# A mixture-of-experts stage whose large and small experts run block by block in turns

## The chip, the cores and the metric

The kernel runs on one core of a Trainium2 chip, as one program. The metric is the time of one execution on the device, in microseconds (us). Before the change three executions took 1911.71, 1914.14 and 1914.71 us.

## What is computed

A network of two blocks over 256 tokens of width 1024: two hybrid attention layers, then two mixer layers, the first with a dense feed-forward part and the last with a mixture of experts. The change touches only that last part:

```python
def swiglu(x, w_gate, w_up, w_down):
    return (jax.nn.silu(x @ w_gate) * (x @ w_up)) @ w_down

def moe_swiglu(x, router_w, w_gate, w_up, w_down):
    logits = (x @ router_w).astype(jnp.float32)
    top_v, top_i = lax.top_k(logits, TOP_K)
    gates = jax.nn.softmax(top_v, axis=-1)
    combine = jnp.sum(jax.nn.one_hot(top_i, N_EXPERTS, dtype=jnp.float32) * gates[..., None], axis=-2)
    y = jnp.zeros_like(x)
    for e in range(N_EXPERTS):
        y = y + combine[..., e:e + 1].astype(x.dtype) * swiglu(x, w_gate[e], w_up[e], w_down[e])
    return y
```

There are 8 experts, each token goes to 2 of them, the inner width is 3584, and all is float32.

## The kernel before, in words

The stage starts some 1000 us into the run, and everything ahead of it stays as it is. The router's counts rank the experts at run time. The program works on eight places `e`: the even ones are large experts (up to 128 tokens), the odd ones small (up to 64, `FEW`). A few tokens too many for their place would go through `overflow`, behind a branch.

The inner width is cut into 7 blocks `b` of 512 columns. A block needs six pieces of weights of 1 MB: two each of gate, up and down. They are loaded by SyncE (SP) in the order of the program (`raw_unit`, L378) into a ring of some 14 buffers, one ahead of the other, each as soon as its buffer's last reader is done.

A large block (`proj`, `down`) keeps float32 accuracy by splitting: `weights` has ScalarE (ACT) round a piece to the high part `whi` (L417, three buffers), and VectorE (DVE) subtract it for the low part (L418). TensorE (PE) then runs three matmuls for each product: L1858, L1859 (high part of the weights with the tokens' high and low part) and L1864 for gate and up; L1932, L1933 and L1935 for down. A small block (`proj_few`, L1877, and the odd branch of `down`, L1918) uses the float32 weights as they come, two matmuls side by side in 64 columns each of the array, with nothing to split.

Between the projections and `down` lies a chain. For a small block ACT copies the result out of PSUM (`act`, L1883), PE transposes it (`turn`, L1893), ACT applies silu (L1898), DVE multiplies (L1899). A large block has silu on ACT (L1885) and a product on DVE (L1886) ahead of the transposes, and a cast on ACT (L1903) and a difference on DVE (L1904) behind them.

`gather` picks an expert's tokens by matmuls with a one-hot matrix (L1767) and copies them to SBUF (`gh`, `gl`; `fx` for the small expert). `scatter` brings an expert's result back to token order (L1951, L1952) and adds it to `y` on DVE (L1954).

The blocks run expert by expert, in one loop over `blocks`; in each step the projections of a block are issued together with `turn` and `down` of the block before. A scheduler in the framework then fixes each engine's order when the program is built, by priorities (`ahead`) and by what it takes to be ready; on the chip each engine keeps that order.

```python
blocks = [(e, b) for e in range(NE) for b in range(7)]
```

Of the kernel before, what the change touches and what calls it, by code (L numbers as in the profile page):

```python
# [11 lines left out]
F32 = mybir.dt.float32  # L12
# [4 lines left out]
ALU = mybir.AluOpType  # L17
# [5 lines left out]
KC = 8  # L23
# [4 lines left out]
NE = 8  # L28
# [3 lines left out]

RANKS = (None, 3, 0, 4, 1, 5, 2, 6)
FEW = 64

SPLITS = (("dsa_q", 256), ("dsa_k", 64), ("dsa_v", 64), ("idx_q", 256), ("idx_k", 32), ("idx_w", 8),
          ("fox_q", 384), ("fox_k", 384), ("fox_v", 384), ("fox_f", 6), ("nsa_q", 384), ("nsa_kc", 128),
# [243 lines left out]
class Net:  # L281
# [1393 lines left out]
    def _moe(self, x, out):  # L1675
        nc, d, hw, tc = self.nc, self.d, self.hw, self.tc
# [63 lines left out]
        def back(oh, dt):  # L1740

            ohf = oh.bitcast(F32) if dt is F32R else oh
            oht = self.late.tile([128, NE, T], dt, name="oht", tag="oht")
            for e in range(0, NE, 2):
                p = self.psum("o")
                for i in range(2):
                    for tb in range(2):
                        t = nc.tensor.transpose(p[:, i * 256 + tb * 128:i * 256 + tb * 128 + 128], ohf[:, tb, e + i], self.ident)
                        self.after(t, gm)
                i = nc.scalar.copy(oht[:, e:e + 2], p.rearrange("p (e t) -> p e t", e=2))  # L1750
                self.after(i, gx)
            return oht

        gh, gl = (own(n).rearrange("p (k s) -> p k s", k=KC) for n in ("gh", "gl"))

        fx = hw.tile([128, KC, FEW], F32, name="fx")

        def gather(qs, tags="ot", low=nc.vector.tensor_copy):

            q = qs[0]  # L1760
            for k in range(0, KC, 2):
                for src, dst, ev, tag in ((xh, gh, nc.scalar.copy, tags[0]), (xl, gl, low, tags[1])):
                    p = self.psum(tag)
                    for i in range(2):
                        for tb in range(2):
                            o = oh[:, tb, q:q + 2] if len(qs) == 2 else oh[:, tb, q][:, None].to_broadcast([128, 2, 128])
                            last = nc.tensor.matmul(p[:, i * 256:i * 256 + 256],  # L1767
                                                    src[:, tb, (k + i) * 128:(k + i) * 128 + 128], o, start=tb == 0,
                                                    stop=tb == 1)
                    p = p.rearrange("p (k s) -> p k s", k=2)  # L1770
                    at = slice(0 if ev == nc.scalar.copy and q else (128 * (q > 0)), 256 if len(qs) == 2 else 128)
                    if at.start < at.stop:
                        kept[ev == nc.vector.tensor_copy] = ev(dst[:, k:k + 2, at], p[:, :, at])
                    if q and src is xl:
                        nc.vector.tensor_tensor(fx[:, k:k + 2], p[:, :, 0:FEW], gh[:, k:k + 2, 0:FEW].bitcast(F32), op=ALU.add)
                yield
            self.hold = kept[0], kept[1] or self.hold[1], None
            kept[2] = last

        b1 = b  # L1780
        early = [[(None, i0)] * 3 + [(None, b)], (None, b)]
        late, kept = kept, [None] * 3
        with self.ahead(5000):
            for _ in gather((0,), ("mm", "mm"), nc.scalar.copy):
                pass
        gx, gm = kept[0], kept[2]
        for cs, p in late:
# [53 lines left out]
        def block_of(n, q, b, hf):  # L1841

            if q == 0:
                return d[n][0, b, hf]
            return d[n][bass.ds(expert[q], 1), b, hf].rearrange("e p n -> (e p) n")
# [2 lines left out]

        def proj(e, b, n, steps=iter(())):

            es = slice(128 * (e > 0), 128 * (e > 0) + 128)
            p = self.psum()
            for hf in range(2):
                w = block_of(n, e, b, hf)
                h, lo = self.weights(w, hold=early.pop(0), pieces=range(4)) if early else self.weights(w)
                for i in range(4):
                    k, cs = hf * 4 + i, slice(i * 512, i * 512 + 512)
                    nc.tensor.matmul(p, gh[:, k, es], h[:, cs], start=k == 0, stop=False)  # L1858
                    nc.tensor.matmul(p, gl[:, k, es], h[:, cs], start=False, stop=False)  # L1859
                if hf:  # L1860
                    next(steps, None)
                for i in range(4):
                    k, cs = hf * 4 + i, slice(i * 512, i * 512 + 512)
                    nc.tensor.matmul(p, gh[:, k, es], lo[:, cs], start=False, stop=k == KC - 1)  # L1864
                next(steps, None) if hf == 0 else None
            PP[e, b, n] = p

        def proj_few(e, b, hf):

            p = PP[e, b] = PP.pop((e, b)) if hf else self.psum()  # L1870
            with self.ahead(3000):
                ws = [self.passing(block_of(n, e, b, hf)) for n in ("mgate", "mup")]
            for i in range(4):
                k = hf * 4 + i
                for r, w in enumerate(ws):
                    r *= FEW
                    nc.tensor.matmul(p[r:r + FEW], fx[:, k], w[:, i * 512:i * 512 + 512], start=k == 0, stop=k == KC - 1,  # L1877
                                     tile_position=(0, r), skip_group_check=True)

        def act(e, b):  # L1880
# [8 lines left out]
        def turn(e, b):  # L1889
            sg = H.pop((e, b))  # L1890
            pt = self.psum("t")
            for i in range(4):
                nc.tensor.transpose(pt[:, i * 128:i * 128 + 128], sg[:, i * 128:i * 128 + 128], self.ident)  # L1893
            if e % 2:
                pv = pt.rearrange("p (f m) -> p f m", f=4)

                fs, fh = sg.rearrange("p (a f m) -> a p f m", a=2, f=4)
                nc.scalar.activation(fs, pv[:, :, 0:FEW], AF.Silu)  # L1898
                nc.vector.tensor_tensor(fh, fs, pv[:, :, FEW:], op=ALU.mult)  # L1899
                H[e, b] = fh  # L1900
                return
            hh, hl = mh[:, (7 * e + b) % 2, 0], mh[:, (7 * e + b) % 2, 1]
            nc.scalar.copy(hh, pt)  # L1903
            nc.vector.tensor_tensor(hl, pt, hh.bitcast(F32), op=ALU.subtract)  # L1904
            H[e, b] = hh, hl

        def down(e, b, steps=iter(())):
            if b == 0:
                YD[e] = [self.psum("s") for _ in range(1 if e % 2 else 2)]
            yd = YD[e]  # L1910
            if e % 2:
                fh = H.pop((e, b))
                for hf in range(2):
                    with self.ahead(3000):
                        w = self.passing(block_of("mdown", e, b, hf))
                    for i, c in product(range(2), range(2)):
                        f, r = hf * 2 + i, FEW * c
                        nc.tensor.matmul(yd[0][r:r + FEW], fh[:, f], w[:, i * 1024 + c * 512:i * 1024 + c * 512 + 512],  # L1918
                                         start=b == 0 and f == 0, stop=b == 6 and f == 3, tile_position=(0, r),
                                         skip_group_check=True)  # L1920
# [20 lines left out]
                self.split(yh, yl, p)  # L1941
                H[e, "y", c] = yh, yl

        def scatter(e, tags="oooo"):
            for c in range(2):
                yh, yl = H.pop((e, "y", c)) if e % 2 == 0 else H[e, "y", 0]
                r = slice(FEW * c, FEW * c + FEW) if e % 2 else slice(0, 128)
# [7 lines left out]
                                                   op1=ALU.add)  # L1955

        mh = None
        blocks = [(e, b) for e in range(NE) for b in range(7)]
        for n, (e, b) in enumerate(blocks):
            if n == 4:  # L1960
                with tc.issue_after(self.load.ins):
                    for q in range(1, NE):
                        r = RANKS[q]
                        expert[q] = nc.values_load(idi[0:1, r:r + 1], engines=(mybir.EngineType.SP,), min_val=1, max_val=NE - 1)
            if n == 9:

                mc = hw.tile([128, 1], F32, name="mc")
# [14 lines left out]
                mh = hw.tile([128, 2, 2, 512], F32R, name="mh", tag="mh")  # L1982
            if n:
                turn(*blocks[n - 1])
            if e % 2:
                proj_few(e, b, 1)
            else:
                if b == 6:
                    steps = gather((e + 1, e + 2)[:NE - 1 - e])
                proj(e, b, "mup", steps)  # L1990
            act(e, b)
            if n:
                down(*blocks[n - 1], steps)
            for _ in steps:
                pass
            if b == 1 and e:
                scatter(e - 1)
            if n == len(blocks) - 5:
                gb = self.rows()
        with self.ahead(4000):  # L2000
            turn(*blocks[-1])
        down(*blocks[-1])
        scatter(NE - 1, ("t", "o", "s", "s"))


        with tc.issue_after(self.load.ins):
# [10 lines left out]
    def rows(self):  # L2017

        nc = self.nc
        r = self.px.tile([1, 2, D], F32, name="rows", tag="x")  # L2020
        nc.gpsimd.dma_start(r, self.d["rows"][None])
        gb = self.xp.tile([128, 2, D], F32, name="gb", tag="xlo")
        for i, c in product(range(2), range(2)):
            p = self.psum("o")
            nc.tensor.matmul(p, self.ones[0:1], r[:, i, c * 512:c * 512 + 512], start=True, stop=True)
            nc.scalar.copy(gb[:, i, c * 512:c * 512 + 512], p)
        return gb
# [112 lines left out]
```

## Time and profile before

| | us |
|---|---|
| median of three executions | 1914.14 |
| profiled execution | 1920.84 |
| its span in the trace | 1919.1 |
| PE busy in the span | 1845.0 (96%) |
| DVE, ACT busy | 1072.9 (56%), 873.5 (46%) |
| loads of weights on SP's queue, share of 16 engines | 66.4% |

Busy times of PE are of pipelined matmuls whose ends are modelled, so that a busy PE need not be at its peak. The granted clock of PE is given as a share of 2.4 GHz; 0.5 of it is the 1.2 GHz level. Each time in the rows below counts from the span's start.

### The profile page before, as it was taken

How to read it: one execution, taken by the hardware profiler on the slowest of the kernel's cores; microseconds unless marked ns; L12 is line 12 of the kernel's file. 1: busy time of each engine (PE TensorE's matmuls, PEld its weight loads, DVE VectorE, ACT ScalarE, POOL GpSimd, SP SyncE). 2: the span in 40 equal slices, each digit the busy share in tenths (PEclk: the TensorE clock that was granted, in tenths of full speed). 3: DMA queues.
4: the chain of work that ended last, by engine and by line, in shares of the span. 5: the costliest groups of instructions: out<-in, count | busy, mean ns of one | idle time of the engine just before them, and what ended most of it. 6: DMA issues, size and time to landing. Idle time of an engine off the chain costs nothing. (4 is left out here: it accounts for less than half of the span.)

```text
span 1919.1 us, 27033 instructions
## 1 busy us (share of the span) xinstructions
PE 1845.0 (96%) x10708; PEld 1363.4 (71%) x10708; DVE 1072.9 (56%) x1582; ACT 873.5 (46%) x1295; POOL 32.9 (2%) x71
## 2 busy tenths in 40 slices
PE   7999999999999999999989999999999999999996
PEld 5777788879888998798877863478436873478532
DVE  3765687765546654555359850388306962278402
ACT  3464465545454543444537740367205751267311
POOL 1000000000000000000000000000000000000000
PEclk9999999999999999899989999999999999999998
DMA  9655443234113555441266989999899999999886
GB/s 390 240 208 198 175 144 111 89 123 154 45 66 132 176 183 190 144 154 48 86 263 253 358 328 390 422 421 401 325 416 422 421 373 360 421 421 415 301 347 258
DMA packets 71173, 497.66 MB, mean 259 GB/s; under 512 B 8226, under 2 KB 9538, under 8 KB 11264
## 3 DMA queue, kind: packets, MB, share of 16 engines
q1 hardware_dynamic: 70752, 495.39, 66.4%
q8 instruction: 86, 1.41, 0.3%
q0 software_dynamic: 288, 0.48, 0.1%
q14 instruction: 47, 0.39, 0.1%
HBM read 493.81 MB, written 1.05 MB: 258 GB/s over the span
## 5 line engine op out<-in xcount | busy, mean ns | idle before, releaser
L418 DVE TENSOR_TENSOR raw<-raw,whi 128x2048 fp32r<-128x2048 f32 (+1 forms) x165 | 297.9, 1823 | 188.8 <-ACT whi L417 187.8
L417 ACT CAST whi<-raw 128x2048 fp32r<-128x2048 f32 (+1 forms) x191 | 292.7, 1557 | 145.8 <-PE mm L439 48.6
L438 PE MATMUL mm<-xhi,whi 128*128 128x256 f32 x720 | 182.1, 288 | 0.7 <-ACT whi L417 0.7
L1858 PE MATMUL mm<-whi,gh 128*128 128x512 f32 x448 | 176.8, 395 | 6.1 <-ACT whi L417 6.1
L417 ACT CAST whi<-room 128x2048 fp32r<-128x2048 f32 (+1 forms) x97 | 171.7, 1804 | 23.5 <-PE mm L1859 7.2
L439 PE MATMUL mm<-xlo,whi 128*128 128x256 f32 x720 | 180.4, 286 | 0.0
L1859 PE MATMUL mm<-whi,gl 128*128 128x512 f32 x448 | 175.6, 392 | 0.0
L1877 PE MATMUL mm<-room,fx 128*64 128x512 f32 x544 | 161.0, 595 | 3.0 <-DMA room<-in_mup_dram 1.8
L418 DVE TENSOR_TENSOR room<-room,whi 128x2048 fp32r<-128x2048 f32 x62 | 142.0, 2290 | 19.5 <-ACT whi L417 16.9
L1899 DVE TENSOR_TENSOR msg<-msg,t 128x256 f32<-128x256 f32 x28 | 11.8, 420 | 237.6 <-ACT msg L1898 237.6
L438 PEld LDWEIGHTS mm<-xhi,whi 128*128 128x128 f32 x720 | 137.6, 191 | 8.1 <-issue 5.6
L439 PEld LDWEIGHTS mm<-xlo,whi 128*128 128x128 f32 x720 | 137.7, 191 | 1.5 <-issue 1.4
L1883 ACT COPY msg<-mm 128x512 f32<-128x512 f32 x28 | 16.4, 585 | 233.3 <-PE mm L1877 233.3
L1877 PEld LDWEIGHTS mm<-room,fx 128*64 128x64 f32 x544 | 48.3, 137 | 87.5 <-issue 79.3
L443 PE MATMUL mm<-xhi,raw 128*128 128x256 f32 x720 | 104.2, 285 | 0.0
L1858 PEld LDWEIGHTS mm<-whi,gh 128*128 128x128 f32 x448 | 84.4, 188 | 27.7 <-ACT whi L417 10.1
L1859 PEld LDWEIGHTS mm<-whi,gl 128*128 128x128 f32 x448 | 84.6, 189 | 17.7
L443 PEld LDWEIGHTS mm<-xhi,raw 128*128 128x128 f32 x720 | 93.6, 191 | 1.2 <-DVE cin L1199 0.9
L1932 PE MATMUL s<-whi,mh 128*128 128x512 f32 x224 | 90.1, 403 | 3.4 <-ACT whi L417 3.4
L1933 PE MATMUL s<-whi,mh 128*128 128x512 f32 x224 | 90.3, 404 | 0.0
L1877 PE MATMUL mm<-raw,fx 128*64 128x512 f32 x232 | 87.1, 609 | 2.3 <-DMA raw<-in_mup_dram 2.3
L1864 PE MATMUL mm<-room,gh 128*128 128x512 f32 x236 | 65.1, 396 | 0.4 <-DVE room L418 0.4
(597 smaller groups left out, 3469.5 us busy)
## 6 DMA issues: line engine op xcount, KB each, us to landing
room<-in_mgate_dram SPq DMA_DIRECT2D x67, 1024.0 KB, 11.4
room<-in_mup_dram SPq DMA_DIRECT2D x64, 1024.0 KB, 10.1
raw<-in_mdown_dram SPq DMA_DIRECT2D x51, 1024.0 KB, 12.1
room<-in_mdown_dram SPq DMA_DIRECT2D x49, 1024.0 KB, 11.7
raw<-in_mup_dram SPq DMA_DIRECT2D x30, 1024.0 KB, 10.2
raw<-in_win_dram SPq DMA_DIRECT2D x29, 1024.0 KB, 6.5
raw<-in_mgate_dram SPq DMA_DIRECT2D x28, 1024.0 KB, 9.4
raw<-in_din_dram SPq DMA_DIRECT2D x24, 1024.0 KB, 4.8
```

The source lines that it names most:

```text
L417: a = nc.scalar.copy(h[:, v], r[:, v])
L418: b = nc.vector.tensor_tensor(lo[:, v], r[:, v], h[:, v].bitcast(F32), op=ALU.subtract)
L438: nc.tensor.matmul(out, w, xh[:, k], start=start and i == 0, stop=False)
L439: nc.tensor.matmul(out, w, xl[:, k], start=False, stop=False)
L443: nc.tensor.matmul(out, lo[:, off + i * 128:off + i * 128 + 128], xh[:, k], start=False, stop=stop and i == n - 1)
L1858: nc.tensor.matmul(p, gh[:, k, es], h[:, cs], start=k == 0, stop=False)
L1859: nc.tensor.matmul(p, gl[:, k, es], h[:, cs], start=False, stop=False)
L1864: nc.tensor.matmul(p, gh[:, k, es], lo[:, cs], start=False, stop=k == KC - 1)
L1877: nc.tensor.matmul(p[r:r + FEW], fx[:, k], w[:, i * 512:i * 512 + 512], start=k == 0, stop=k == KC - 1, tile_position=(0, r), skip_group_c ...
L1883: nc.scalar.copy(sg, PP.pop((e, b)))
L1932: nc.tensor.matmul(yd[c], hh[:, fs], h[:, ws], start=b == 0 and f == 0, stop=False)
L1933: nc.tensor.matmul(yd[c], hl[:, fs], h[:, ws], start=False, stop=False)
```

## The change

Large and small experts are paired: after two blocks of the first large expert, a small block and a large block follow in turns until the end. What goes with it: the small experts' tokens `fx` get two buffers, a large expert always uses the first half of `gh`, the small experts' `down` accumulates in the PSUM bank `o`, and `gather`, `scatter`, `back` and `rows` use the four shared banks `mm` in place of `o` and `t`. The registers with the experts' numbers are loaded at the second block and not at the fifth. No matmul, cast or load is added or left out.

```diff
+BEHIND = 2
...
-        def gather(qs, tags="ot", low=nc.vector.tensor_copy):
+        FX = {}
+        def gather(q, tags="mm", low=nc.vector.tensor_copy, some=True, few=True):
+            if few:
+                fx = FX[q + 1] = hw.tile([128, KC, FEW], F32, name="fx", tag="fx", bufs=2)
+            at = slice(0 if some else 128, 256 if few else 128)
...
-            es = slice(128 * (e > 0), 128 * (e > 0) + 128)
+            es = slice(0, 128)
...
         def down(e, b, steps=iter(())):
             if b == 0:
-                YD[e] = [self.psum("s") for _ in range(1 if e % 2 else 2)]
+                YD[e] = [self.psum("o")] if e % 2 else [self.psum("s") for _ in range(2)]
...
-        def scatter(e, tags="oooo"):
+        def scatter(e, tags=("mm",) * 4):
...
-        blocks = [(e, b) for e in range(NE) for b in range(7)]
+        many, few = ([(e, b) for e in range(i, NE, 2) for b in range(7)] for i in range(2))
+        blocks = many[:BEHIND]
+        for i in range(len(few)):
+            blocks += [few[i], *many[BEHIND + i:BEHIND + i + 1]]
         for n, (e, b) in enumerate(blocks):
-            if n == 4:
-                with tc.issue_after(self.load.ins):
-                    for q in range(1, NE):
+            if n == 1:
+                for q in range(1, NE):
...
+            if n + 1 == BEHIND:
+                steps = gather(0, some=False)
...
-                if b == 6:
-                    steps = gather((e + 1, e + 2)[:NE - 1 - e])
+                if b == 6 and e + 2 < NE:
+                    steps = gather(e + 2)
...
-            if b == 1 and e:
-                scatter(e - 1)
+            if n > 2 and blocks[n - 2][1] == 6:
+                scatter(blocks[n - 2][0])
```

First place: PE around the transposes of a small block, in a run of small blocks before. `fx` marks the projections, `msg` with 64 columns `down`, `lead` the transposes.

```order
L1877 MATMUL mm<-x,fx 64x512
L1877 MATMUL mm<-raw_10976,fx 64x512
L1918 MATMUL s<-raw_10988,msg 64x512 x4
L1893 MATMUL t<-lead,msg 128x128 x4
L1918 MATMUL s<-raw_10994,msg 64x512 x4
L1877 MATMUL mm<-room_11001,fx 64x512
```

The same place after the change, where the lines stand some ten further down: `room_10897` and `room_10899` are the last weights of a small block's projections, L1943, L1944 and L1946 the `down` of the large block before it.

```order
L1886 MATMUL mm<-room_10897,fx 64x512
L1886 MATMUL mm<-room_10899,fx 64x512
L1902 MATMUL t<-lead,msg 128x128 x4
L1943 MATMUL s<-whi,mh 128x512
L1944 MATMUL s<-whi,mh 128x512
```

Four matmuls of `down` stood between a small block's last projection and its transposes; now nothing does, and the large block's `down` comes behind them.

Second place: ACT in a run of small blocks before.

```order
L1883 COPY msg<-mm 128x512
L1898 ACTIVATE msg<-t 128x256
L1883 COPY msg<-mm 128x512
L1898 ACTIVATE msg<-t 128x256
L417 CAST whi<-room_11185 128x2048
```

ACT after the change, one pair of blocks: the last two casts of a large block's up weights, its silu and the cast behind its transposes, then the small block's copy, and on either side of the small block's silu the casts of the large block's down weights.

```order
L418 CAST whi<-xlo 128x2048
L418 CAST whi<-raw_10844 128x2048
L1894 ACTIVATE msg<-mm 128x512
L1913 CAST mh<-t 128x512
L1892 COPY msg<-mm 128x512
L418 CAST whi<-x 128x2048
L1907 ACTIVATE msg<-t 128x256
L418 CAST whi<-raw_10929 128x2048
```

The casts that the large block's `down` waits for have come to stand behind a copy that waits for the small block's last projection. This holds for 26 of the 28 pairs.

Third place: PE at the end of a large block's up projection after the change. L1867, L1868 and L1873 are the three products, L1929 is the `down` of the small block before.

```order
L1867 MATMUL mm<-whi,gh 128x512
L1868 MATMUL mm<-whi,gl 128x512
L1929 MATMUL o<-raw_10865,msg 64x512
L1873 MATMUL mm<-xlo,gh 128x512 x4
L1929 MATMUL o<-raw_10865,msg 64x512 x3
L1929 MATMUL o<-room_10871,msg 64x512 x4
```

One of the eight matmuls of the small `down` is cut off from the other seven by the low products; this stands 22 times in the program. Before, a run of small blocks kept the eight in two fours.

## Rows read from the trace of the kernel before

**Rows 1.** The page, part 1: busy us (share of span) x instructions of each engine.

```profile
PE 1845.0 (96%) x10708; PEld 1363.4 (71%) x10708; DVE 1072.9 (56%) x1582; ACT 873.5 (46%) x1295; POOL 32.9 (2%) x71
```

**Rows 2.** Busy time by stretch: stretch, its length, each engine, then PE clock, DMA share, GB/s.

```profile
1262.34:1330.13 67.79, 67.79 (x305) 55.62 (x304) 60.74 (x33) 48.55 (x32) 0.00 (x0) 1.00 1.01 417
1384.76:1428.91 44.15, 44.15 (x210) 15.11 (x209) 1.68 (x4) 3.87 (x8) 0.00 (x0) 1.00 1.01 417
...
1262.34:1484.33 221.99, 214.89 (x946) 131.17 (x944) 117.60 (x83) 95.47 (x77) 0.00 (x0) 0.99 0.98 395
```

**Rows 3.** Waits of PE from 1000 us on: total us, times, longest.

```profile
PE o L1951 <- DVE y L1954: 6.3, 7, 0.9
PE mm L1858 <- ACT whi L417: 6.1, 5, 1.6
PE s L1932 <- ACT whi L417: 3.4, 3, 1.1
PE t L1893 <- ACT msg L1883: 2.8, 4, 0.7
PE mm L1877 <- DMA raw<-in_mup_dram: 2.3, 2, 1.4
PE mm L1877 <- DMA room<-in_mup_dram: 1.8, 2, 0.9
```

**Rows 4.** Timeline of PE, change to the last small expert: start, us, work, [idle before <-releaser].

```profile
1803.25 1.02 PE L1877 MATMUL mm<-room,fx 128*64 128x512 f32 x2
1804.95 0.66 PE L1893 MATMUL t<-lead,msg 128*128 128x128 f32 x4 [0.68 <-ACT msg L1883]
1806.75 0.50 PE L1932 MATMUL s<-whi,mh 128*128 128x512 f32 x1 [1.14 <-ACT whi L417]
...
1809.07 1.20 PE L1935 MATMUL s<-xlo,mh 128*128 128x512 f32 x4 [0.19 <-DVE xlo L418]
1810.11 0.40 PE L1932 MATMUL s<-whi,mh 128*128 128x512 f32 x1
```

**Rows 5.** Timeline of ACT, the same place.

```profile
1804.31 0.59 ACT L1883 COPY msg<-mm 128x512 f32<-128x512 f32 x1 [6.43 <-PE mm L1877]
1804.79 1.90 ACT L417 CAST whi<-room 128x2048 fp32r<-128x2048 f32 x1
```

**Rows 6.** Timeline of PE, change to the second small expert.

```profile
1355.68 3.65 PE L1877 MATMUL mm<-room,fx 128*64 128x512 f32 x16
1360.05 0.66 PE L1893 MATMUL t<-lead,msg 128*128 128x128 f32 x4 [0.71 <-ACT msg L1883]
...
1366.30 0.40 PE L1932 MATMUL s<-whi,mh 128*128 128x512 f32 x1
...
1384.76 0.66 PE L1893 MATMUL t<-lead,msg 128*128 128x128 f32 x4
```

**Rows 7.** Stretches behind three such changes, PE alone: granted clock, DMA share, GB/s.

```profile
1807.00:1810.00 3.00, 2.81 (x12) 1.00 0.80 298
...
1362.00:1365.00 3.00, 3.00 (x8) 0.52 0.98 396
1585.00:1587.00 2.00, 2.00 (x6) 0.50 0.98 397
```

**Rows 8.** Timeline of PE, change from a small to a large expert.

```profile
1232.89 0.39 PE L1859 MATMUL mm<-whi,gl 128*128 128x512 f32 x1
1233.21 1.07 PE L1918 MATMUL s<-room,msg 128*64 128x512 f32 x2
1234.21 1.20 PE L1864 MATMUL mm<-room,gh 128*128 128x512 f32 x4
...
1238.91 0.66 PE L1893 MATMUL t<-lead,msg 128*128 128x128 f32 x4
```

**Rows 9.** Timeline of PE, down of the last small block.

```profile
1894.96 3.22 PE L1918 MATMUL s<-room,msg 128*64 128x512 f32 x13
```

**Rows 10.** Timeline of DVE: the experts' numbers become ready.

```profile
1018.16 0.17 DVE L1829 CAST idi<-ids 128x7 int32<-128x7 f32 x1
```

More of the change, by code (lines that the diff above doesn't have):

```diff
@@ L1744, in back @@
             for e in range(0, NE, 2):
-                p = self.psum("o")
+                p = self.psum()
                 for i in range(2):
@@ L1754, in _moe @@
         gh, gl = (own(n).rearrange("p (k s) -> p k s", k=KC) for n in ("gh", "gl"))
-        fx = hw.tile([128, KC, FEW], F32, name="fx")
-        def gather(qs, tags="ot", low=nc.vector.tensor_copy):
-            q = qs[0]
+        FX = {}
[3 more added lines that the diff above has]
+            at = slice(0 if some else 128, 256 if few else 128)
             for k in range(0, KC, 2):
-                for src, dst, ev, tag in ((xh, gh, nc.scalar.copy, tags[0]), (xl, gl, low, tags[1])):
+                for src, dst, ev, tag in ((xh, gh, nc.scalar.copy, tags), (xl, gl, low, tags)):
                     p = self.psum(tag)
@@ L1765, in gather @@
                         for tb in range(2):
-                            o = oh[:, tb, q:q + 2] if len(qs) == 2 else oh[:, tb, q][:, None].to_broadcast([128, 2, 128])
+                            o = oh[:, tb, q:q + 2] if few else oh[:, tb, q][:, None].to_broadcast([128, 2, 128])
                             last = nc.tensor.matmul(p[:, i * 256:i * 256 + 256],
@@ L1770, in gather @@
                     p = p.rearrange("p (k s) -> p k s", k=2)
[L1771 to L1775, printed above, removed]
-                yield
-            self.hold = kept[0], kept[1] or self.hold[1], None
-            kept[2] = last
+                    if src is xh:
+                        a = ev(gh[:, k:k + 2, at], p[:, :, at])
+                    else:
+                        if some:
+                            b = ev(gl[:, k:k + 2, 0:128], p[:, :, 0:128])
+                        if few:
+                            nc.vector.tensor_tensor(fx[:, k:k + 2], p[:, :, 128:128 + FEW],
+                                                    gh[:, k:k + 2, 128:128 + FEW].bitcast(F32), op=ALU.add)
+                yield
+            if some:
+                if low == nc.scalar.copy:
+                    a, b = b, None
+                self.hold = a, b or self.hold[1], None
+                kept[:] = a, b, last
         b1 = b
@@ L1783, in _moe @@
         with self.ahead(5000):
-            for _ in gather((0,), ("mm", "mm"), nc.scalar.copy):
+            for _ in gather(0, low=nc.scalar.copy, few=False):
                 pass
@@ L1876, in proj_few @@
                     r *= FEW
-                    nc.tensor.matmul(p[r:r + FEW], fx[:, k], w[:, i * 512:i * 512 + 512], start=k == 0, stop=k == KC - 1,
+                    nc.tensor.matmul(p[r:r + FEW], FX[e][:, k], w[:, i * 512:i * 512 + 512], start=k == 0, stop=k == KC - 1,
                                      tile_position=(0, r), skip_group_check=True)
@@ L1901, in turn @@
                 return
-            hh, hl = mh[:, (7 * e + b) % 2, 0], mh[:, (7 * e + b) % 2, 1]
+            i = (7 * (e // 2) + b) % 2
+            hh, hl = mh[:, i, 0], mh[:, i, 1]
             nc.scalar.copy(hh, pt)
@@ L1915, in down @@
                         w = self.passing(block_of("mdown", e, b, hf))
+                    next(steps, None)
                     for i, c in product(range(2), range(2)):
@@ L1957, in _moe @@
         mh = None
-        blocks = [(e, b) for e in range(NE) for b in range(7)]
+        many, few = ([(e, b) for e in range(i, NE, 2) for b in range(7)] for i in range(2))
+        blocks = many[:BEHIND]
+        for i in range(len(few)):
+            blocks += [few[i], *many[BEHIND + i:BEHIND + i + 1]]
         for n, (e, b) in enumerate(blocks):
-            if n == 4:
-                with tc.issue_after(self.load.ins):
-                    for q in range(1, NE):
-                        r = RANKS[q]
-                        expert[q] = nc.values_load(idi[0:1, r:r + 1], engines=(mybir.EngineType.SP,), min_val=1, max_val=NE - 1)
+            if n == 1:
+                for q in range(1, NE):
+                    r = RANKS[q]
+                    expert[q] = nc.values_load(idi[0:1, r:r + 1], engines=(mybir.EngineType.SP,), min_val=1, max_val=NE - 1)
             if n == 9:
@@ L2002, in _moe @@
         down(*blocks[-1])
-        scatter(NE - 1, ("t", "o", "s", "s"))
+        scatter(NE - 1, ("t", "mm", "s", "s"))
         with tc.issue_after(self.load.ins):
@@ L2023, in rows @@
         for i, c in product(range(2), range(2)):
-            p = self.psum("o")
+            p = self.psum()
             nc.tensor.matmul(p, self.ones[0:1], r[:, i, c * 512:c * 512 + 512], start=True, stop=True)
```

## Prediction

> **What bounds the kernel now.** Read the page first: PE is busy for 96% of the span [rows 1]. That is a mean over very different stages, so the second look is at stretches of the expert stage, cut where PE starts the transposes of a block [rows 2]. Four large blocks take 67.79 us, 16.95 us each. Four small blocks take 44.15 us, 11.04 us each. PE has no idle moment in either, and the transfers run at 417 GB/s in both. A block needs six pieces of 1 MB, 6.29 MB in all, which take 15.1 us at 417 GB/s. So a large block is slower than its loads by 1.9 us, a small one faster than its loads by 4.1 us; the ring of buffers carries this over, and at the changes between experts one or the other runs out. The third row is a whole pair of experts, 221.99 us for seven large and seven small blocks: 7 x (16.95 + 11.04) = 195.9 us of block work, and 26 us for gathering, scattering and losses.
>
> The third look is at what PE waits for [rows 3]. The waits are small: weights from DMA, or casts that wait for them, and `scatter`'s single PSUM bank. But two rows, the third and the fourth, come from a pattern worth following, because the change repeats it. At the change from a large to a small expert PE finishes the small block's projections, then wants to transpose their result and has nothing else in line.
>
> **The price of that pattern.** In the timeline the projections end at 1803.25 + 1.02 = 1804.27 [rows 4]. The transposes wait 0.68 us, because ACT must first copy the result, from 1804.31 for 0.59 us [rows 5]. Behind the copy ACT starts the cast for the large block's `down` (1.90 us), and PE waits 1.14 us more, later 0.19 us for the low part. The second half of `down` starts at 1810.11. Between lie four transposes (0.6 us) and twelve wide matmuls at 0.23 us (a large block's 16.95 us over its 72 and its transposes), 3.4 us of work. So the pattern loses 5.84 - 3.4 = 2.4 us.
>
> It can cost more. At another change the same rows run from 1355.68 + 3.65 = 1359.33 to 1366.30, 6.97 us [rows 6]: 1.1 us more, because the granted clock right behind the waits is 0.52, the 1.2 GHz level. Of three such changes it fell to that level at two, and stayed at 2.4 GHz at one [rows 7].
>
> **What the change adds.** The pattern now stands in 26 of 28 pairs of blocks, as the first two places of the order show: before, four matmuls of `down` between a small block's projection and its transposes hid ACT's copy, and in a run of small blocks there was no cast to wait for. Three cases existed, so 23 are new: 23 x 2.4 = 55 us. Nothing can fill these waits, because PE's and ACT's orders are fixed in the program. The clock I let fall in half the cases, 13 against 2 before: 11 x 1.1 = 12 us. The bounds are none more (0) and all 26 (24 x 1.1 = 26 us).
>
> The third place, a single small matmul cut off from its seven fellows, is there before too, at the changes from a small to a large expert [rows 8]. From 1232.89 to 1238.91 are 6.02 us for one wide matmul, four low products and eight matmuls of `down`. In a run eight small ones take 3.65 us [rows 6], so uncut it would be 0.23 + 0.92 + 3.65 = 4.8 us; the cut loses 1.2 us. The row shows where: alone, the call takes 1.0 us to the next start, while in a run two share the array's halves. 22 such cuts against 3 before are 19 x 1.2 = 23 us. The Trainium skill has a rule on this, in TensorEngine Tiling (Array Packing), Key Properties: changing the tiling mode drains the engine. The row agrees that a switch costs something: the small call starts 0.32 us behind a matmul that otherwise yields after 0.23, some 0.1 us. By that rule alone a cut, two switches, would cost 0.2 us and all of them 4 us in place of 23, and the forecast would be 1960.
>
> **What the change takes away.** With the loads evened out, the waits for weights go: 6.1 + 2.3 + 1.8 = 10 us. `scatter` has four banks in place of one, so 6.3 us go [rows 3]. And in the stretch behind a large expert the scatter was strewn among small matmuls: from 1360.05 to 1384.76 are 24.7 us [rows 6] for transposes (0.6), a large `down` (24 x 0.23 = 5.5), sixteen small projections (7.3), half a small `down` (1.8) and eight scatter matmuls (1.8), 17.0 us of work. Of the other 7.7 us I count 2.3 as the pattern and 0.9 as a bank wait; of the 4.5 left half should go, since seven of the eight scatter matmuls now stand in one row: 4 x 2.2 = 9 us, between 0 and 18.
>
> **What costs nothing.** The registers with the experts' numbers are now read ahead of the eleventh load, which so waits until 1018.16 [rows 10]; six loads that ran before that are held up. What covers them is the first two large blocks, 34 us of work on pieces loaded earlier, ahead of the small block that needs the first four. Those land 10 us after they start at 417 GB/s. If the cover were gone, PE would lose some 10 us once. A pair of blocks needs 30.2 us of transfers, and PE now takes 16.95 + 11.04 + 2.4 + 1.2 = 31.6 us for it, so the loads stay ahead. The gathers make as many matmuls and copies as before; sharing four banks with projections may cost or save a few us, and I take zero.
>
> **The sum.** 55 + 12 + 23 = 90 us added, 10 + 6 + 9 = 25 us taken away: 65 us slower. The profiled execution took 1920.84 us, so 1986; the median of the runs lies 6.7 us lower, so **1979 us**. With no more falls of the clock and cuts at the price of a switch it is 1948; with all falls and no gain at the scatters it is 1979 + 14 + 9 = 2002, and with 8 us lost in gathers 2010. That is this case's own range.
>
> **Rivals.** *The loads set the pace* and it is faster. For it: the pieces of a pair need only 30.2 us, against 31.7 us per pair of blocks now (221.99 / 7), and small and large blocks balance. 326 pieces behind 1018.16 take 326 x 1.0486 MB / 417 GB/s = 820 us; the last small `down` then starts at 1838 in place of 1894.96 and 24 us follow it [rows 9]: 1862 us of span, 1857 on the runs' median. It decides where PE needs under 30.2 us a pair, that is, loses under 2.2 us in pattern and cut together. Against it: the pattern alone loses 2.4, and it is a matter of order, not of speed. The Trainium skill speaks for this rival, in Trainium Kernel Development and Optimization, Performance Expectations: matmul busy time is a bad measure, weight loading's share a good one. The trace has 131.17 us of weight loading in the pair's 221.99, 59%, which by that rule leaves PE much room [rows 2].
>
> *Half the price*: the scheduled order hides part of the waits or cuts. Half of 90 us is 45, and the time 1934, with a tail down to 1905.
>
> *Waits in series*: while PE stands, buffers stay taken and the loads stop too. Then a pair costs 30.2 + 2.4 + 1.2 = 33.8 us, 2.2 us over the 31.6 above, 28 times: 62 us more, 2040. Against it: the ring holds more than two blocks.
>
> **Chances.** Forecast 0.72, loads' pace 0.12, half the price 0.10, waits in series 0.06. A measurement of this kernel can tell about 0.2% (4 us) from no change. Faster by more than that: 0.12 and 0.02 of the half price, 0.14; within: 0.04; slower: 0.82. The range 1915 to 2010 holds the forecast's own range and most of the half price; the loads' pace and the series are left out.
>
> **What would show it.** In the profile after, PE should wait about 26 x 0.7 = 18 us for the small block's copy and 26 x 1.14 = 30 us for the cast of `down`, in the rows that now read 2.8 and 3.4; waits for DMA should be all but gone; a pair of blocks should take 32 us; transfers should run near 400 GB/s throughout. The clock should dip in many places. The prediction is wrong if PE waits for DMA at most blocks (the loads' pace), or if a pair takes under 31 us.

## The result and the profile after

The changed kernel takes 1980.77 us, the median of four runs (1974.61 to 1983.07), against 1913.7 us for the kernel before beside it. The ratio is 1.0347 with a 95% interval of 1.0322 to 1.0372: 67 us slower. The forecast was 1979. The profiled execution took 1974.61 us, span 1972.8.

The page of the changed kernel, its heading and part 1:

```profile
span 1972.8 us, 27011 instructions
...
PE 1871.3 (95%) x10708; PEld 1363.1 (69%) x10708; DVE 1072.1 (54%) x1582; ACT 870.3 (44%) x1295; POOL 32.9 (2%) x71
```

The number of PE instructions is that of [rows 1], 10708. No work was added, only time between instructions. PE's share of busy time fell by one point only, so the page's first part alone would tell little; the waits say in front of which instructions the time lies.

The waits of PE from 1000 us on (total us, times, longest):

```profile
PE s L1943 <- ACT whi L418: 29.7, 26, 1.1
PE t L1902 <- ACT msg L1892: 18.9, 27, 0.7
PE t L1902 <- DVE msg L1895: 1.6, 1, 1.6
PE s L1946 <- DVE raw L419: 1.4, 7, 0.2
PE s L1946 <- DVE room L419: 1.2, 6, 0.2
PE mm L1962 <- DVE y L1965: 1.1, 3, 0.4
```

The first two are the rows that read 3.4 us x 3 and 2.8 us x 4 in [rows 3]. They grew in number and not in size. No row for DMA is left, and `scatter`'s wait is down from 6.3 to 1.1.

The timeline of PE at one of the 26 patterns, with the cut ahead of it (a call on half of the columns, as at line 1929, leaves two records in the trace, so x2 is one call; a matmul of a large block leaves one):

```profile
1362.97 0.39 PE L1868 MATMUL mm<-whi,gl 128*128 128x512 f32 x1
1363.29 1.07 PE L1929 MATMUL o<-raw,msg 128*64 128x512 f32 x2
1364.29 1.20 PE L1873 MATMUL mm<-raw,gh 128*128 128x512 f32 x4
1365.41 1.50 PE L1929 MATMUL o<-raw,msg 128*64 128x512 f32 x5
...
1368.99 0.66 PE L1902 MATMUL t<-lead,msg 128*128 128x128 f32 x4
1369.58 7.09 PE L1886 MATMUL mm<-room,fx 128*64 128x512 f32 x32
1377.38 0.66 PE L1902 MATMUL t<-lead,msg 128*128 128x128 f32 x4 [0.71 <-ACT msg L1892]
1379.17 0.50 PE L1943 MATMUL s<-whi,mh 128*128 128x512 f32 x1 [1.14 <-ACT whi L418]
...
1381.50 1.20 PE L1946 MATMUL s<-x,mh 128*128 128x512 f32 x4 [0.19 <-DVE x L419]
```

The timeline of ACT at the same place:

```profile
1376.74 0.59 ACT L1892 COPY msg<-mm 128x512 f32<-128x512 f32 x1 [6.47 <-PE mm L1886]
1377.22 1.90 ACT L418 CAST whi<-raw 128x2048 fp32r<-128x2048 f32 x1
```

ACT had stood for 6.47 us, with the cast next in its order behind a copy that could not start before PE was through. PE then waits for the copy and for the cast: 0.71 + 1.14 + 0.19 = 2.04 us. That is [rows 4, 5] over again, in 26 of the 28 pairs of blocks.

Busy time by stretch in the changed kernel (length, engines, PE clock, DMA share, GB/s): a pair of blocks with no fall of the clock, one with a fall, and the place of that fall:

```profile
1377.38:1409.55 32.17, 30.13 (x129) 17.56 (x129) 15.37 (x9) 12.99 (x11) 0.00 (x0) 1.00 0.98 391
1106.91:1140.19 33.28, 31.42 (x128) 18.82 (x129) 15.37 (x9) 13.09 (x11) 0.00 (x0) 0.95 0.94 360
1109.00:1112.00 3.00, 3.00 (x9) 2.30 (x9) 3.00 (x3) 3.00 (x2) 0.00 (x0) 0.53 1.00 418
```

A pair takes 32.17 us, and 1.1 us more where the granted clock falls to the 1.2 GHz level (0.53). Looked through in stretches of 1 us from 1001 us on, and leaving out the very end, where every kernel here has one, this execution has 9 such falls: 8 at the 26 patterns, each some 2 us behind the transposes, and one at 1884 us, where the last rows are read. The profiled execution of the kernel before has 5, two of them at its three patterns.

### The profile page after: what moved, and what is told of

It reads as the page before. It is cut to its first block, busy times and chain, and to the rows that moved or that the text cites. A ratio compares the mean times of both kernels' runs of the same rounds, so it can differ in the third digit from the quotient of the medians.

```text
span 1972.8 us, 27011 instructions
## 1 busy us (share of the span) xinstructions
PE 1871.3 (95%) x10708; PEld 1363.1 (69%) x10708; DVE 1072.1 (54%) x1582; ACT 870.3 (44%) x1295; POOL 32.9 (2%) x71
## 5 line engine op out<-in xcount | busy, mean ns | idle before, releaser
L419 DVE TENSOR_TENSOR raw<-raw,whi 128x2048 fp32r<-128x2048 f32 (+1 forms) x163 | 293.3, 1817 | 215.5 <-ACT whi L418 198.0
L418 ACT CAST whi<-raw 128x2048 fp32r<-128x2048 f32 (+1 forms) x211 | 331.0, 1591 | 140.3 <-PE mm L440 48.6
L1886 PE MATMUL mm<-room,fx 128*64 128x512 f32 x816 | 202.9, 599 | 0.0
L1867 PE MATMUL mm<-whi,gh 128*128 128x512 f32 x448 | 175.2, 391 | 0.0
L1868 PE MATMUL mm<-whi,gl 128*128 128x512 f32 x448 | 174.7, 390 | 0.0
L1886 PEld LDWEIGHTS mm<-room,fx 128*64 128x64 f32 x816 | 60.7, 138 | 109.4 <-issue 107.2
L1943 PE MATMUL s<-whi,mh 128*128 128x512 f32 x224 | 96.8, 433 | 29.7 <-ACT whi L418 29.7
L1913 ACT CAST mh<-t 128x512 fp32r<-128x512 f32 x28 | 16.4, 585 | 237.3 <-PE t L1902 237.3
L418 ACT CAST whi<-room 128x2048 fp32r<-128x2048 f32 (+1 forms) x63 | 107.8, 1746 | 12.4 <-PE mm L1868 6.0
L1867 PEld LDWEIGHTS mm<-whi,gh 128*128 128x128 f32 x448 | 84.1, 188 | 19.0 <-ACT whi L418 1.3
L1868 PEld LDWEIGHTS mm<-whi,gl 128*128 128x128 f32 x448 | 84.2, 188 | 17.7
L1944 PE MATMUL s<-whi,mh 128*128 128x512 f32 x224 | 94.5, 423 | 0.0
L419 DVE TENSOR_TENSOR room<-room,whi 128x2048 fp32r<-128x2048 f32 x30 | 68.7, 2291 | 44.6 <-ACT whi L418 43.2
L1929 PE MATMUL o<-room,msg 128*64 128x512 f32 x248 | 78.3, 596 | 0.0
L1943 PEld LDWEIGHTS s<-whi,mh 128*128 128x128 f32 x224 | 44.7, 200 | 46.4 <-ACT whi L418 35.8
```

The costliest lines, as they stand in the source:

```text
L418: a = nc.scalar.copy(h[:, v], r[:, v])
L419: b = nc.vector.tensor_tensor(lo[:, v], r[:, v], h[:, v].bitcast(F32), op=ALU.subtract)
L1886: nc.tensor.matmul(p[r:r + FEW], FX[e][:, k], w[:, i * 512:i * 512 + 512], start=k == 0, stop=k == KC - 1, tile_position=(0, r), skip_grou ...
L1943: nc.tensor.matmul(yd[c], hh[:, fs], h[:, ws], start=b == 0 and f == 0, stop=False)
L1944: nc.tensor.matmul(yd[c], hl[:, fs], h[:, ws], start=False, stop=False)
```

## Experiments

Each run is beside the kernel before on the same chip. The theory is that of the prediction: order alone costs the time. The rivals put it on the turns as such, that is on loads, buffers, changes of mode or the other edits.

| run | median us | ratio to before, 95% interval |
|---|---|---|
| the change | 1980.77 | 1.0347 (1.0322 to 1.0372) |
| uncut | 1945.55 | 1.0157 (1.013 to 1.0183) |
| cut_by_two | 1960.45 | 1.0213 (1.0198 to 1.0227) |
| transposes_late | 2004.45 | 1.0457 (1.0431 to 1.0483) |
| casts_early | 1900.2 | 0.9923 (0.9898 to 0.9947) |
| all_three | 1879.83 | 0.9809 (0.9789 to 0.983) |
| whole_experts | 1909.56 | 0.9971 (0.9958 to 0.9984) |
| whole_experts_cured | 1893.87 | 0.9887 (0.9868 to 0.9905) |
| filled_wait | 1973.2 | 1.0292 (1.0269 to 1.0315) |

**uncut.** The eight calls at line 1929 are held behind `low_last`, the last matmul of line 1873. Only the first of them stood ahead of it, so only that one moves.

```diff
-                        nc.tensor.matmul(yd[0][r:r + FEW], fh[:, f], ...)
+                        m = nc.tensor.matmul(yd[0][r:r + FEW], fh[:, f], ...)
+                        self.after(m, self.low_last)
```

> The first small down matmul is ordered behind the last low product of the large up projection, so the eight stand in one row; nothing else is held. Theory (a lone call on half the columns takes 1.0 us, and a cut costs 1.2 us): 22 cuts x 1.2 = 26 us less than the changed kernel's 1980.8, so about 1955, ratio 1.021 to the kernel before. Rival (a cut costs two switches of 0.1 us): 4 us less, 1976. Rival (the waits swallow it, since ACT or the loads set the pace): 1980.

Measured: 1945.55 us, 35 less than the change. The timeline of PE in uncut:

```profile
1356.44 0.39 PE L1868 MATMUL mm<-whi,gl 128*128 128x512 f32 x1
1356.67 1.07 PE L1873 MATMUL mm<-raw,gh 128*128 128x512 f32 x4
1357.66 1.94 PE L1929 MATMUL o<-raw,msg 128*64 128x512 f32 x8
1359.43 1.89 PE L1929 MATMUL o<-room,msg 128*64 128x512 f32 x8
1361.25 0.66 PE L1902 MATMUL t<-lead,msg 128*128 128x128 f32 x4
```

From the last wide matmul to the transposes are 4.81 us here and 6.02 in the change (1362.97 to 1368.99), so a cut costs 1.21 us, and 22 of them 27 us. PE's two waits are the same to 0.1 us, so nothing swallowed the gain. The waits of PE in uncut, the first two rows:

```profile
PE s L1944 <- ACT whi L418: 29.7, 26, 1.1
PE t L1902 <- ACT msg L1892: 18.9, 27, 0.7
```

The clock falls 5 times in place of 9, some 4 us by the pair rows. The other 4 us lie inside the two intervals (5 us each way).

**cut_by_two.** This asks what the price of a cut is made of. Two calls go ahead of the low products, one on each half of the columns, and six follow. `down` becomes a generator that `proj` steps (`halves` is set then), so that the two are issued inside it.

```diff
-                    nc.tensor.matmul(p, gh[:, k, es], lo[:, cs], ...)
+                    m = nc.tensor.matmul(p, gh[:, k, es], lo[:, cs], ...)
+                    if hf and self.pair:
+                        self.after(m, self.pair)
+                        self.low_last = m
...
+                        if halves and (hf, i) == (0, 1):
+                            yield
...
+                        if halves and hf == i == 0:
+                            self.pair = m
+                        elif halves:
+                            self.after(m, self.low_last)
```

> In the changed kernel two small down matmuls, one on each half of the columns, stand ahead of the four low products, where one stood; six follow. Two changes of mode remain at each cut. Theory (the price is the lone call, whose other half of the columns stands empty; twice in a cut of 1 and 7): the cut falls from 1.24 us (pair 32.17 against 30.93 in uncut) to 0.1 to 0.3, so a pair takes 31.1 us and the time is 1950 to 1957. Rival (the price is the change of mode, or low products that stand behind): a pair stays at 32.1 or so, 1975 to 1981.

Measured: 1960.45 us on a chip where the kernel before took 1919.1; by the ratios that is 26 us less than the change, 1955, where the theory had put it and far from the rival. A pair takes 31.32 us for the 31.1 expected, 0.85 less than in the change; 22 such gains are 19 us, and the other 7 of the 26 are not accounted for, though they are little more than the two intervals allow. Busy time by stretch in cut_by_two, a pair without a fall:

```profile
1372.36:1403.68 31.32, 29.25 (x128) 17.29 (x128) 15.38 (x9) 12.98 (x11) 0.00 (x0) 1.00 1.00 403
```

The timeline of PE in cut_by_two:

```profile
1358.79 0.39 PE L1869 MATMUL mm<-whi,gl 128*128 128x512 f32 x1
1359.11 1.08 PE L1938 MATMUL o<-raw,msg 128*64 128x512 f32 x4
1360.12 1.20 PE L1874 MATMUL mm<-raw,gh 128*128 128x512 f32 x4
1361.24 1.08 PE L1938 MATMUL o<-raw,msg 128*64 128x512 f32 x4
...
1363.97 0.66 PE L1906 MATMUL t<-lead,msg 128*128 128x128 f32 x4
```

Two calls hold PE from 1359.11 to 1360.12, 1.01 us; in the change one call holds it from 1363.29 to 1364.29, 1.00 us. The six behind take 1361.24 to 1363.97, 2.73 us; the seven of the change take 1365.41 to 1368.99, 3.58 us, as long as uncut's eight (1357.66 to 1361.25, 3.59 us). An odd call costs as much as two, on both sides of the cut. The whole stretch is 5.18 us, so of the 1.21 us some 0.84 are the odd calls and 0.37 the rest, a little over the 0.1 to 0.3 expected: changes of mode and the starts around them, which no run here tells apart. The Trainium skill's rule (TensorEngine Tiling (Array Packing), Key Properties: changing the tiling mode drains the engine) fits the 0.37; the larger part is one that this rule doesn't speak of.

**transposes_late.** The small block's transposes are ordered behind the large block's `down`; ACT's order stays.

```diff
-                nc.tensor.transpose(pt[:, i * 128:i * 128 + 128], ...)
+                t = nc.tensor.transpose(pt[:, i * 128:i * 128 + 128], ...)
+                if e % 2:
+                    self.after(t, self.down_last)
```

> The small block's transposes are ordered behind the large block's down; ACT's order is left alone. Theory (ACT's copy and then its cast stand ahead of down; the transposes only sit in that shadow): the two waits become one of about 0.68 + 0.6 + 1.14 = 2.4 us in front of down, and the four transposes' 0.6 us come on top: 1981 to 1996, no gain, and PE waits for the cast of down in place of both rows. Rival (the early transposes are what costs): 26 x 0.68 = 18 us less, 1963.

Measured: 2004.45 us, slower than the change and above the theory's own bound of 1996. The waits of PE in transposes_late, the first row:

```profile
PE s L1945 <- ACT whi L418: 65.1, 26, 2.5
```

Busy time by stretch in transposes_late, a pair without a fall and one of the falls:

```profile
1317.24:1349.84 32.60, 29.90 (x130) 17.54 (x129) 15.47 (x9) 12.89 (x10) 0.00 (x0) 1.00 0.97 385
1394.00:1397.00 3.00, 3.00 (x9) 2.32 (x8) 2.91 (x2) 3.00 (x2) 0.00 (x0) 0.50 1.01 426
```

The two waits did become one of 2.5 us, as the theory says, and the rival falls: taking the transposes out of the way gains nothing while ACT copies first. A pair without a fall is 0.43 us longer, 11 us in 26. What the expectation had missed is the clock: it fell at 22 of the 26 patterns in place of 8, and 14 falls at 1.1 us are 15 us. Together 26 us, for 24 measured.

**casts_early.** The other side of the same place: the first half of `down` is loaded and cast before the small block's copy, and the first matmuls of `down` are ordered behind the small projections (`few_last`).

```diff
-                nc.scalar.copy(sg, PP.pop((e, b)))
+                self.after(nc.scalar.copy(sg, PP.pop((e, b))), self.parted[0])
...
-                    h, lo = self.weights(block_of("mdown", e, b, hf))
+                    h, lo = pre.pop(0) if pre else self.weights(block_of("mdown", e, b, hf))
...
             if e % 2:
+                pre[:] = [self.weights(block_of("mdown", *blocks[n - 1], hf)) for hf in range(1)]
                 proj_few(e, b, 1)
```

> The first half of the large block's down is loaded and cast ahead of the small block's copy on ACT, and down starts right behind the small projections; the transposes fall behind down by themselves. The cuts stay. Theory: the pattern's 26 x 2.4 = 62 us and the 10 falls of the clock (11 us) go; a pair would need 32.2 - 2.4 = 29.8 us of PE, and the loads' 30.2 us begin to tell: 1905 to 1930, no row of waits for the copy, waits for the cast near 2 us. Rival (the waits come from turns between large and small as such, from loads or buffers): they turn up elsewhere, 1960 to 1981.

Measured: 1900.2 us, 81 less than the change and faster than the kernel before, with the blocks still by turns and the cuts still there. The timeline of ACT in casts_early:

```profile
1352.54 1.90 ACT L418 CAST whi<-raw 128x2048 fp32r<-128x2048 f32 x1
1359.09 0.59 ACT L1893 COPY msg<-mm 128x512 f32<-128x512 f32 x1 [4.64 <-PE mm L1887]
```

The timeline of PE in casts_early, the same place, where no wait stands; the last row shows the transposes:

```profile
1351.95 7.09 PE L1887 MATMUL mm<-room,fx 128*64 128x512 f32 x32
1358.97 0.50 PE L1944 MATMUL s<-whi,mh 128*128 128x512 f32 x1
...
1363.74 0.49 PE L1903 MATMUL t<-lead,msg 128*128 128x128 f32 x3
```

Busy time by stretch in casts_early, a pair:

```profile
1334.18:1363.74 29.56, 29.56 (x130) 17.57 (x129) 15.47 (x10) 12.88 (x11) 0.00 (x0) 1.00 1.01 420
```

ACT now uses the time for which it stood idle to cast. A pair fell from 32.17 to 29.56, so the pattern costs 2.6 us. 26 x 2.6 = 68 us and the 8 falls at the patterns, all gone, at 1.1 us make 77 of the 81.

Three things go with this run. The time is below the 1905 expected: a pair takes less than the 30.2 us that its pieces need at 417 GB/s, and still no row of PE's waits names DMA. And PE's order has changed with ACT's, since the transposes now stand behind nearly all of `down`. So the run prices the early cast and this move together; transposes_late shows that the move alone gains nothing, and the early cast alone was not tried. The kernel also loads and casts one piece at its end that nothing reads, as all_three does.

**all_three.** The three edits above in one kernel.

> Casts early, transposes behind down, and no cut, blocks still by turns. Theory: 62 + 11 + 26 = 99 us less than 1980.8 would be 1882; the loads' 30.2 us a pair are now above PE's 28.6, which takes some of it back: 1875 to 1900, faster than the kernel before (1914) by 1 to 2%. PE's waits are then for DMA, the clock hardly falls. Rival (turns cost by themselves): above 1914.

Measured: 1879.83 us, 2% faster than the kernel before (ratio 0.9809, 0.9789 to 0.983) and 5% faster than the change. Busy time by stretch in all_three, a pair of blocks and two pairs of experts:

```profile
1323.85:1352.38 28.53, 28.53 (x130) 17.43 (x128) 15.46 (x10) 12.87 (x10) 0.00 (x0) 1.00 1.01 422
1187.27:1399.33 212.06, 211.65 (x945) 128.76 (x944) 117.90 (x82) 94.02 (x77) 0.00 (x0) 1.00 1.00 411
1399.33:1611.47 212.14, 211.73 (x945) 128.77 (x945) 117.91 (x82) 94.01 (x77) 0.00 (x0) 1.00 1.00 416
```

A pair takes 28.53 us, the sum of a large and a small block in [rows 2] (16.95 + 11.04 = 27.99) and half a microsecond. A pair of experts takes 212.1 us against 221.99 before. One guess in the expectation was wrong: PE does not wait for loads, no row of its waits names DMA. Seven pairs are 7 x 28.53 = 199.7 us, and gathers and scatters add 12 us of PE. The 84 pieces of 1.0486 MB need 209 us at the pair's 422 GB/s, and the DMA share is 1.00 over the whole stretch. PE and the loads are level, and the clock doesn't fall once from 1001 us until PE's work ends.

**whole_experts** and **whole_experts_cured.** The order of the blocks undone, all other edits of the change kept, without and with the three cures.

```diff
-        blocks = many[:BEHIND]
-        for i in range(len(few)):
-            blocks += [few[i], *many[BEHIND + i:BEHIND + i + 1]]
+        blocks = [(e, b) for e in range(NE) for b in range(7)]
```

> The changed kernel with the blocks again in the order of whole experts; its other edits (early register load, four banks for scatter and gathers, two buffers of gathered tokens) stay. Theory (all of the loss is the order): the 26 patterns and 22 cuts fall back to 3 each, and what remains of the edits saves the scatter's bank waits (6 us) and costs nothing: 1895 to 1914. Rival (the early register load or the shared banks cost): above 1920.

> Whole experts as in the run before it, with the three cures of all_three (casts early, transposes behind down, no cut). Theory: the cures find only 3 patterns (7 us) and 3 cuts (4 us) here, so 5 to 15 us less than whole_experts, 1885 to 1905; what is then left between this and all_three's 1880 is what the turns bring by themselves, the waits for weights (10 us in the kernel before). Rival (the turns bring nothing): within 4 us of 1880.

Measured: 1909.56 and 1893.87 us. The first is 0.3% faster than the kernel before (ratio 0.9971, 0.9958 to 0.9984), 5 us. The wait for `scatter`'s bank, 6.3 us in [rows 3], is gone from its waits, and PE waits for no weights at the start of the stage, so the register load has no visible price. But the waits for a cast ahead of a large block's projections, 6.1 us in [rows 3], are 12.1 here. So the other edits together cost nothing and the order of the blocks alone makes the 71 us between 1909.56 and 1980.77. The second shows what is left for the turns to take away; the waits of PE in whole_experts_cured:

```profile
PE mm L1868 <- ACT whi L418: 12.1, 6, 2.5
PE t L1903 <- DVE msg L1896: 2.7, 1, 2.7
PE mm L1887 <- DMA room<-in_mup_dram: 2.5, 3, 1.3
PE mm L1887 <- DMA raw<-in_mup_dram: 1.4, 1, 1.4
```

The timeline of ACT in whole_experts_cured, at the end of a small expert:

```profile
1233.22 0.58 ACT L532 CAST my<-o 128x512 fp32r<-128x512 f32 x1 [7.34 <-PE o L1932]
1233.80 0.58 ACT L1916 CAST mh<-t 128x512 fp32r<-128x512 f32 x1
1234.28 1.90 ACT L418 CAST whi<-room 128x2048 fp32r<-128x2048 f32 x1
```

The timeline of PE at the same place:

```profile
1236.23 0.50 PE L1868 MATMUL mm<-whi,gh 128*128 128x512 f32 x1 [2.47 <-ACT whi L418]
```

Three of the six waits in the first row are these, 2.47 us each: ACT stood for 7.34 us, with the cast of the small expert's result (`my`) next in its order, which waits for PE; the cast of weights that PE wants next comes behind it. That is not a wait for loads but the pattern of the change at another place. The other three, 4.7 us, and the last two rows, 3.9, are waits for weights, 8.6 us, as [rows 3] had 10; in all_three all of them are gone. The turns are worth 1893.87 - 1879.83 = 14 us, once their own waits are gone, and by these rows an estimate is that half of them are owed to evened-out loads.

**filled_wait.** The small block's transposes are made three times over with the same result, which gives PE work while the cast runs.

```diff
-            for i in range(4):
+            for i in range(4 * (3 if e % 2 else 1)):
+                i %= 4
```

> In the changed kernel the small block's four transposes are made three times over, with the same result; nothing else. The eight more (about 1.2 us) fill PE's wait for the cast of down. Theory (the clock falls because PE stands, and that is a cost beside the waits): waits for the cast fall from 29.7 us to under 5, the 9 falls go or nearly so, and the time falls by 8 to 15 us though PE does more work: 1966 to 1973. Rival (falls come with the stage's work, whatever the waits): 9 falls stay, 1978 to 1985.

Measured: 1973.2 us, 8 us less by the medians and 11 by the ratios, with more work for PE. The timeline of PE in filled_wait:

```profile
1349.96 1.53 PE L1903 MATMUL t<-lead,msg 128*128 128x128 f32 x12 [0.71 <-ACT msg L1892]
1351.77 0.50 PE L1944 MATMUL s<-whi,mh 128*128 128x512 f32 x1 [0.28 <-ACT whi L418]
```

Busy time by stretch in filled_wait, a pair:

```profile
1349.96:1382.13 32.17, 30.99 (x136) 18.45 (x137) 15.37 (x9) 12.99 (x11) 0.00 (x0) 1.00 0.98 390
```

A pair takes 32.17 us, to the hundredth what it took. Yet none of the 8 falls at the patterns is left; one stays at 1883 us, and one stands at the start of the stage, which the change's profiled execution did not have. Eight falls at 1.1 us are 9 us. The falls at the patterns belong to PE's standing and are a cost beside it. The wait for the cast is 7.1 us in all, a little over the bound of 5.

## Why the prediction was right

The signs that the prediction named are there: the two rows of waits, none for DMA, a pair of 32.17 us for 32, 391 GB/s for 400, and dips of the clock.

**The pattern (+55).** Right in place and count, and nearly in size. The two waits came out as 18.9 and 29.7 us where 18 and 30 were forecast, and casts_early puts the whole pattern at 2.6 us for the 2.4 taken: 23 x 2.6 = 60.

**The clock (+12).** Right in kind, too large: 8 falls and not 13 at the patterns, so 6 are new and not 11, 7 us at 1.1 each. These are counts of one execution; uncut, with the same waits, had 5. filled_wait shows that the term exists, apart from the waits.

**The cut (+23).** 1.21 us measured for 1.2, 19 x 1.21 = 23. The reason was half told: the lone call pays once, and the seven behind it pay again, since seven take as long as eight. The case in which a cut costs only its switches (0.2 us) falls by the 1.21 us; what cut_by_two leaves of it without the odd calls is 0.37.

**What goes (-25).** All three terms together are 5 us by whole_experts and 14 by the pair of cured kernels, 19. How this splits into banks, waits for weights and strewn scatters is not shown: in whole_experts the bank's 6.3 us go and 7.4 us of waits behind ACT's order come.

**What costs nothing.** whole_experts carries the early register load and the shared banks, and its time shows no price of either.

**The sum.** 60 + 7 + 23 - 19 = 71 us for the 67 measured, whose interval is 5 us each way; the prediction had 65. The pattern was 5 us too small, the falls 5 too large and the gains 6 too large. The mechanism was right; that these errors nearly cancel, so that 1979 lies within 2 us of 1980.77, is luck, and the 4 us between 71 and 67 lie within the interval.

**The rivals.** "The loads set the pace" names a gain that lay behind the pattern: all_three meets its condition of under 2.2 us lost per pair (28.53 against 27.99), and is faster than the kernel before. That the loads then set the pace is not shown, since PE waits for none of them. The rival's 1857 is too low by 23 us. Its span of 1862 is 12 short of the 1874.0 profiled: busy time by stretch in all_three, from 1018.16 us to the 1838 where the rival has the loads end, shows 413 GB/s and not 417, which is 8 us over 326 pieces; the other 4 stay open.

```profile
1018.16:1838.00 819.84, 817.06 (x3641) 496.61 (x3641) 447.96 (x327) 361.32 (x301) 0.58 (x1) 1.00 1.00 413
```

The other 11 us are the step from the profiled span to the median, 5 us down in the kernel before and 6 us up in all_three. "Half the price" falls by 2.6 and 1.21 us, both at full price, and "waits in series" by the pair of 32.17 us, for which it had 33.8.

The share of weight loading told little here. In all_three it is 128.77 of 212.14 us, 61%, in a stretch in which PE stands for 0.4 us and the DMA share is 1.00; before it was 59% [rows 2]. The Trainium skill (Trainium Kernel Development and Optimization, Performance Expectations) prefers this share, beside the share of peak arithmetic, to matmul busy time. By it PE would have room here. The trace shows none to use while the loads stay as they are; whether PE's matmuls could follow each other faster no run shows.

## What to carry to other kernels

Before work is interleaved more finely, look at what happens once at each present change of kind, price it from the timeline, and multiply by the new number of changes. When an engine waits for a conversion, look at what stands ahead of it in that engine's order: ACT had been idle for 6.5 us before the cast that PE waited for. Putting the cast ahead of one copy, with PE's transposes falling behind `down`, was worth 81 us, while moving the transposes alone cost 24. The same pattern stands in whole_experts_cured behind another cast, in a row that reads like a wait for weights: what ACT did before the cast tells the two apart. Keep calls that use half the array in even runs.

## What the runs showed that was not expected

A call on half the columns without a partner takes as long as two, at either side of the cut: 1.00 us for one, 1.01 for two, 3.58 for seven, 3.59 for eight.

In these executions, one of each kernel, the granted clock fell the more often the longer PE stood at one place. With 0.71 and then 0.28 us of standing it fell at none of 26 patterns, with 0.71 and 1.14 at 8 (5 in uncut, 8 in cut_by_two), with 2.5 us in one piece at 22. The fall at the start of the stage is a matter of its own: the profiled executions that have it (transposes_late, casts_early, filled_wait) reach the first transposes of the stage at 1031.9 to 1033.3 us, those without it (the change, uncut, all_three, cut_by_two) at 1026.9 to 1027.7. That is some 5 us in executions of kernels whose program is nearly the same up to there, and it may be why the change's profiled execution lies 6 us under its median; what decides it was not tried.
